# Two tiles' places inside the last output projection, four conditioning steps and the state outputs sooner, another slot ring

## The chip, the core and the metric

The kernel runs on one core of one Trainium2 chip. The metric is the device time of one execution in microseconds (us): 667.77 us is the median of 3 runs of the kernel before (667.08 to 668.85). Engines are named as in the profile: PE (TensorE; PEld is its weight load), DVE (VectorE), ACT (ScalarE), POOL (GpSimd) and SP (SyncE, which issues most of the DMAs).

## The reference

One layer of a hybrid decoder for 256 prompt tokens and 64 sample tokens, all in 32-bit floats: a conditioned projection, two groups of mixing heads, an output projection with a norm behind it, and a mixture of 32 experts of which every token uses two.

```python
def hybrid_layer(x, c, h0, conv0, w_ada, b_ada, ...):
    mod = jax.nn.silu(c) @ w_ada + b_ada
    sh1, sc1, g1, sh2, sc2, g2 = jnp.split(mod[:, None, :], 6, axis=-1)
    h = x * (1.0 + sc1) + sh1
    u, v, xr, yr = jnp.split(h @ w_in, [...], axis=-1)
    v = layer_norm(v, lnv_g, lnv_b)
    out_a = gmlp_spatial(u, v, w_s, b_s)
    xc, conv_new = causal_conv(xr, conv0, conv_w, conv_b)
    hs, h_last = rglru(xc, h0, lru_wa, lru_ba, lru_wx, lru_bx, lru_lam)
    mix = jnp.concatenate([out_a, hs * jax.nn.gelu(yr)], axis=-1) @ w_out
    x = layer_norm(ALPHA * x + (1.0 + g1) * mix, ln1_g, ln1_b)
    h = x * (1.0 + sc2) + sh2
    x = layer_norm(ALPHA * x + (1.0 + g2) * hier_moe(h, ...), ln2_g, ln2_b)
    return x, h_last, conv_new, v

def hier_moe(x, w_rg, b_rg, w_re, b_re, w1, w3, w2):
    gsel = argmax(x @ w_rg + b_rg)                # one group of 8 experts per token
    topv, topi = lax.top_k(le_sel, TOP_K)         # two experts in that group
    wk = softmax(topv) * pgsel
    for e in range(32):
        acc += gate[:, e] * ((silu(x @ w1[e]) * (x @ w3[e])) @ w2[e])
```

The width is 1024, an expert is 512 wide, so its three matrices are 6 MB and all of them 192 MB.

## The kernel before

**Tiles.** The tokens are three tiles: t = 0 and 1 are 128 prompt tokens each, t = 2 the 64 sample tokens. All buffers of weights are 1 MB "slots" of two rings (`slots[0]` with 9, `slots[1]` with 8); a tile that is allocated takes the next buffer of its ring and its first writer waits for the last reader of the tile that was there. PSUM is a ring of 8 banks.

**Order.** The order of every engine's instructions is the order in which the code is written (a manual schedule), and each engine works through its own in order. A wait at one instruction so holds everything behind it on that engine. SP issues the loads of weights in the order of the code too, each when its slot is free.

**Stages around the change.** (1) The projections u, v, xr, yr (L352), with the conditioning of groups 0 to 2 (`ada`, L175) between them. Then the state outputs: four transposes exT (L598), a copy on ACT into a part of a buffer called gx, and four DMA issues on POOL. (2) The output projection, `out_proj(t, n2s)` (L646 on, matmuls L656 and L660): for each tile two halves of 512 columns, eight k each; DVE adds the residual (L664 to L667). (3) `norm(t)` on DVE (L673 to L685) makes the rows h2, whose last step for each half is L682; `turn_h2(t, h)` transposes them on PE (L693), ACT copies them out; `logits(t)` (L703) multiplies with the router's weights; `logits_end` (L707) and `route` (L737 to L751) on DVE pick two experts per token and leave a 0/1 matrix M of token by expert. (4) `count(t)`: two matmuls on M (L763, L764) give, per token and expert, how many tokens came before it, in a PSUM bank pn. `arrange(t)` on DVE (L769 to L775) turns that into places and builds the 0/1 matrix Pd of token by place. `sort(t)` (L857) multiplies h2 with Pd, eight matmuls of 128 columns for tile 2 and of 256 columns for the others (the trace counts two passes for each), and so puts the tokens in the order of their experts; `sorted_out(t)` copies the PSUM banks to xD, in turns on ACT and DVE (L844, L846). (5) `ranks` and "most" (L779 to L887): the largest number of tokens of any expert, which every engine loads into a register. `fetch(0)` copies the first experts' windows xT from xD (L930). All engines then branch on "most" (`tc.If`, L1106). (6) The experts: up (L958), down (L982), combination (L1000). They walk over 200 loads of weights ("we", L639), of which 15 are issued ahead of the branch.

**The last conditioning.** Group 3 (g2, needed only at the very end) has its four loads of two steps each issued in `load_ada2(3)` at L198, its eight steps of four matmuls run by `ada_some(n)` (L175) and its end `ada_end(3)` (L186) on DVE ahead of the branch. `Pd` lies in a slot called "pd" of ring 1, whose first write is a memset of a 128-column strip (L757).

The order of the code from the output projection on, before:

```python
out_proj(2); whiten[2] = norm(2); out_proj(0)
turn_h2(2, 0); turn_h2(2, 1); whiten[0] = norm(0)
out_proj(1, (0,)); logits(2); turn_h2(0, ...); logits(0); route(0 and 2)
out_proj(1, (1,)); count(2); count(0); whiten[1] = norm(1)
ada_some(8); arrange(2); arrange(0)
turn_h2(1, ...); logits(1); logits_end(1); route(1)
sort(2); sort(0, (0, 2)); count(1); sort(0, (4, 6)); arrange(1)
sorted_out(2); sorted_out(0); sort(1); ranks; most; sorted_out(1); ada_end(3)
fetch(0); tc.If(...)
```

Of the kernel before, what the change touches and what calls it, by code (L numbers as in the profile page):

```python
# [17 lines left out]
NE = 32  # L18
# [19 lines left out]
def hymba_step(tc, I, O):  # L38
    nc = tc.nc
    with ExitStack() as ctx:  # L40
# [9 lines left out]
        def slot(name, shape=(128, 2048), dt=F32, i=0):  # L50
            return slots[i].tile(list(shape), dt, name=name, tag="w")
# [50 lines left out]
        gx_ = slot("gx")  # L102
# [90 lines left out]

        def load_ada2(g):
            r = []
            for c in range(4):
                w = slot("wada", (128, 2, 1024))
                nc.sync.dma_start(w, wada[2 * c:2 * c + 2, :, 1024 * (g + 2):1024 * (g + 3)].rearrange("k p n -> p k n"))  # L198
                r += [(2 * c, w[:, 0, :]), (2 * c + 1, w[:, 1, :])]
            return r  # L200
# [321 lines left out]
        for t in range(3):  # L522
# [12 lines left out]
            dst = uT[:, :, TOFF[t]:TOFF[t] + n]  # L535
            V.tensor_tensor(dst, dst, tm, op=OP.mult)
        mb = {}
        mbs = [slot(f"mb{i}", i=1) for i in range(2)]
# [56 lines left out]
        wo = [load_half(wout, 0), load_half(wout, 1)]  # L595
        pex = bank("exT", (36, 512))
        for c in range(4):
            T.transpose(pex[:, c * 128:(c + 1) * 128], ex[:, c, :], ident)  # L598
        exo = gx_[0:36, 1536:2048]
        S.copy(exo, pex)  # L600

        G.dma_start(O["new_h_prompt"][0], exo[0:1, :])
        G.dma_start(O["new_h_sample"][0], exo[1:9, :])
        G.dma_start(O["new_conv_prompt"].rearrange("l b k c -> (l b k) c"), exo[9:12, :])
        G.dma_start(O["new_conv_sample"].rearrange("l b k c -> (l b k) c"), exo[12:36, :])

        G.iota(io256, pattern=[[1, 256]], base=0, channel_multiplier=0, allow_small_or_imprecise_dtypes=True)
# [33 lines left out]
        load_until(4)  # L641
        w_g2 = load_ada2(3)
        V.memset(lg[64:128, 2, :], 0.0)
        st1 = {}

        def out_proj(t, n2s=(0, 1)):  # L646
            n = TW[t]
# [3 lines left out]
            for n2 in n2s:  # L651
                cs = slice(n2 * 512, n2 * 512 + 512)
                p = bank("po")
                if t < 2:
                    for k in range(8):
                        T.matmul(p, abT[k // 4][:, k % 4, ts], wo[n2][k // 4][:, k % 4, :], start=(k == 0), stop=(k == 7))  # L656
                else:
                    for k in range(4):
# [99 lines left out]
        pn = {}  # L758

        def count(t):  # L760

            pn[t] = bank("pn", (128, 2, NE))
            T.matmul(pn[t][:, 0, :], before, M[:, t, :], start=True, stop=True)  # L763
            T.matmul(pn[t][:, 1, :], ones, M[:, t, :], start=True, stop=True)  # L764
# [48 lines left out]
        whiten[2] = norm(2)  # L813
        out_proj(0)
        turn_h2(2, 0)
# [9 lines left out]
        route(slice(0, 3, 2))  # L825
        out_proj(1, (1,))
        count(2)
        count(0)
        whiten[1] = norm(1)
        ada_some(8)  # L830
        arrange(2)
        arrange(0)
        turn_h2(1, 0)
        turn_h2(1, 1)
        logits(1, range(8))


# [22 lines left out]
        def sorted_out(t):  # L860
            W = WID[t]
            per = 512 // W
            for k0 in range(0, 8, per):
                evac(xD[:, k0:k0 + per, XO[t]:XO[t] + W], sorted_.pop((t, k0)))

        logits_end(1)
        route(slice(1, 2))
# [4 lines left out]
        gD = exp.tile([128, NP], F32, name="gD")  # L872
        sort(2)
        sort(0, (0, 2))
        count(1)
        sort(0, (4, 6))
        arrange(1)
        for PT in PT2:
            for cs in (slice(256, 320), slice(384, 448)):
                V.tensor_scalar(PT[:, cs], ident[:, 0:64], 0.0, None, op0=OP.mult)  # L880
        sorted_out(2)
        sorted_out(0)
# [12 lines left out]
        sorted_out(1)  # L895
        ada_end(3)

# [206 lines left out]
        fetch(0)  # L1104
        first = xg[0][1]
        with tc.If(n_most > CAP):  # L1106
            gates_and_windows()
# [165 lines left out]
```

## Time and profile before

| what | value |
|---|---|
| median of 3 runs | 667.77 us (667.08 to 668.85) |
| the profiled execution | 670.56 us |
| its span | 668.7 us |
| PE busy | 591.6 us, 88% |
| DVE busy | 273.0 us, 41% |
| ACT busy | 126.6 us, 19% |
| POOL busy | 52.7 us, 8% |
| DMA, mean | 364 GB/s over the span, 243.57 MB |
| chain of waits | DMA 59%, PE 9%, POOL 1%, DVE 1% |

The page of the profile has one line per engine with its busy time, the span in 40 slices, the chain of work that ended last, and the groups of instructions that cost most. A busy share is a mean over stages with different limits; the chain of waits says which engine or transfer released the next piece of the work that ended last, and the rows of a stretch show what one engine did there, when, and what ended an idle time ahead of it. [...]

### The profile page before, as it was taken

To read this page: it belongs to the slowest core of one execution; us is meant where nothing else is said; L and a number is where in the kernel's file an instruction comes from. 1 tells how busy PE (TensorE), PEld (TensorE's weight loads), DVE (VectorE), ACT (ScalarE), POOL (GpSimd) and SP (SyncE) were. 2 spreads that over 40 slices of the span, in tenths; PEclk is the share of its full clock that TensorE was granted. 3 is DMA by queue.
4 is the path that set the end of the run, shared out by engine and by line. 5 is a ranking of instruction groups with operands and counts; after the bars stand their busy time and mean duration, and the time that the engine had idled before them with its cause. 6 is when DMAs were issued, how large, how long until landed. Compare 5 with 4: busy or idle time off the path is not lost.

```text
span 668.7 us, 7628 instructions
## 1 busy us (share of the span) xinstructions
PE 591.6 (88%) x2767; PEld 271.7 (41%) x2767; DVE 273.0 (41%) x742; ACT 126.6 (19%) x216; POOL 52.7 (8%) x81
## 2 busy tenths in 40 slices
PE   4579999999989999999988989897988979899990
PEld 1377688545743344343332324233332323233330
DVE  0198567694672323323253233232223152323435
ACT  0156371110121101101111111111101010112211
POOL 2031405400000000000010000000000010200003
PEclk9779999999699999999999999999999999999996
DMA  8998859926969999999999999999999999999922
GB/s 328 378 327 311 301 155 311 364 72 240 422 260 419 420 422 421 420 420 420 422 420 421 420 422 421 420 420 421 420 422 420 423 420 421 420 421 421 404 97 79
DMA packets 43949, 243.57 MB, mean 364 GB/s; under 512 B 5678, under 2 KB 6422, under 8 KB 17794
## 3 DMA queue, kind: packets, MB, share of 16 engines
q1 hardware_dynamic: 43106, 242.58, 90.3%
q0 software_dynamic: 800, 0.45, 0.4%
q8 instruction: 23, 0.38, 0.2%
q14 instruction: 20, 0.16, 0.1%
HBM read 241.49 MB, written 1.52 MB: 363 GB/s over the span
## 4 chain that ended last, share of the span: by engine, by line
DMA 59%; PE 9%; POOL 1%; DVE 1%; issue 0%; POOLq 0%; ACT 0%; ACTq 0%; SPq 0%
DMA we<-in_w 59%; PE p L958 6%; PE p L1185 1%; PE pc L1175 1%; POOL xk L1236 0%; PE pc L1000 0%; PE pc L1199 0%; POOLq L1269 0%; POOL xk L1237 0%; PE pgd L908 0%; DVE st L1209 0%; PE ph L970 0%; PE pc L1197 0%; PE pc L1004 0%; PE pr L948 0%
## 5 line engine op out<-in xcount | busy, mean ns | idle before, releaser
L958 PE MATMUL p<-we,xT 128*64 128x512 f32 x1024 | 240.6, 597 | 29.1 <-DMA we<-in_w 26.8
L958 PEld LDWEIGHTS p<-we,xT 128*64 128x64 f32 x1024 | 73.3, 136 | 174.6 <-issue 124.7
L982 PE MATMUL p<-we,hT 128*64 128x512 f32 x480 | 110.0, 596 | 8.0 <-DMA we<-in_w 6.2
L986 DVE TENSOR_TENSOR y<-p,y 64x512 fp32r<-64x512 f32 x60 | 41.3, 689 | 76.7 <-ACT y L985 76.7
L963 ACT ACTIVATE s<-p 64x512 f32<-64x512 f32 x32 | 18.9, 589 | 274.6 <-PE p L958 274.6
L964 DVE TENSOR_TENSOR h<-p,s 64x512 f32<-64x512 f32 x32 | 22.2, 694 | 117.7 <-ACT s L963 117.3
L982 PEld LDWEIGHTS p<-we,hT 128*64 128x64 f32 x480 | 33.5, 137 | 81.4 <-issue 53.2
L930 DVE COPY xT<-xD 128x192 f32 (+1 forms) x96 | 23.6, 248 | 92.7 <-PE p L958 79.0
L985 ACT CAST y<-p 64x512 fp32r<-64x512 f32 x60 | 34.8, 579 | 104.1 <-PE p L982 79.7
L175 PE MATMUL ada<-wada,md 128*32 128x512 f32 (+1 forms) x256 | 27.2, 534 | 6.7 <-DMA wada<-in_w_ada 5.0
L1000 PE MATMUL pc<-y,PT 128*128 128x512 f32 x120 | 32.2, 408 | 0.4 <-DVE y L986 0.2
L1000 PEld LDWEIGHTS pc<-y,PT 128*128 128x128 f32 x120 | 21.3, 188 | 16.4 <-issue 11.4
L352 PE MATMUL pf<-hH,whi 128*128 128x320 f32 x64 | 20.6, 322 | 0.0
L352 PE MATMUL pf<-hL,whi 128*128 128x320 f32 x64 | 19.8, 309 | 0.0
L352 PE MATMUL pf<-hH,wlo 128*128 128x320 f32 x64 | 19.7, 308 | 0.0
L509 POOL PARTITION_BROADCAST g2k<-mod x4 | 1.8, 548 | 196.9 <-PE p L958 196.9
L1004 PE MATMUL pc<-y,PT 128*128 128x512 f32 x60 | 16.2, 392 | 0.0
L656 PE MATMUL po<-wq,uT 128*128 128x512 f32 x32 | 14.7, 601 | 0.0
L857 PE MATMUL px<-pd,h 128*128 128x256 f32 (+1 forms) x48 | 14.4, 471 | 0.1
L656 PE MATMUL po<-wq,ga 128*128 128x512 f32 x32 | 14.4, 592 | 0.0
L970 PEld LDWEIGHTS ph<-ident,h 128*128 128x128 f32 x64 | 9.0, 209 | 12.0 <-issue 7.9
L293 DVE TENSOR_TENSOR wlo<-wq,whi 128x1024 fp32r<-128x1024 f32 x12 | 13.9, 1218 | 0.0
(323 smaller groups left out, 586.5 us busy)
## 6 DMA issues: line engine op xcount, KB each, us to landing
we<-in_w SPq DMA_DIRECT2D x188, 1024.0 KB, 19.8
wada<-in_w_ada SPq DMA_DIRECT2D x24, 1024.0 KB, 5.3
wq<-in_w_in SPq DMA_DIRECT2D x8, 1024.0 KB, 9.2
wq<-in_w_out SPq DMA_DIRECT2D x4, 1024.0 KB, 5.4
we<-in_w SPq DMA_DIRECT2D x8, 512.0 KB, 11.5
xk<-in_x_prompt SPq DMA_DIRECT2D x1, 1024.0 KB
out_y_prompt<-xk SPq DMA_DIRECT2D x4, 256.0 KB
xk<-in_x_sample SPq DMA_DIRECT2D x1, 256.0 KB
```

The lines of the kernel that those rows point to most:

```text
L175: T.matmul(ada_p[g][32 * j:32 * j + 32, :], cT[:, k, :], wj, start=(k == 0), stop=(k == 7))
L352: T.matmul(p, w[k // 4][part][:, k % 4, f * 128:(f + 1) * 128], x[:, k, :], start=(i == 0 and k == 0), stop=(i == 2 and k == 7))
L656: T.matmul(p, abT[k // 4][:, k % 4, ts], wo[n2][k // 4][:, k % 4, :], start=(k == 0), stop=(k == 7))
L930: V.tensor_copy(xT[:, :, BASE[t]:BASE[t] + CAPS[t]], xD[:, :, XO[t]:XO[t] + WID[t] + CAPS[t]][:, :, bass.ds(v, CAPS[t])])
L958: T.matmul(p[64 * q:64 * q + 64, :], xT[:, k, :], w(q, k), start=(k == 0), stop=(k == 7))
L963: S.activation(s[64:128, :], p[0:64, :], AF.Silu)
L964: V.tensor_tensor(h[64 * a:64 * a + 64, :], p[64:128, :], s[64:128, :], op=OP.mult)
L982: T.matmul(p[q], hT[:, k, sl], w(q, k), start=(k == 0), stop=(k == 3))
L985: S.copy(yg[0][sl, cs], p[q])
L986: V.tensor_tensor(yg[1][sl, cs], p[q], yg[0][sl, cs].bitcast(F32), op=OP.subtract)
L1000: T.matmul(pc[t, q], PT[:, TOFF[t]:TOFF[t] + 128], yg[i][:, H[q]], start=False, stop=stop and i == 1)
L1004: T.matmul(pc[2], PT[:, cs], yg[i][:, H[q]], start=False, stop=False)
```

## The change

Six things change, and no arithmetic. (a) The four exT transposes, their copy and the four state outputs are written ahead of the last projection rather than behind it; the last quarter of the output weights thereby takes the buffer gx. (b) `load_ada2(3, 1)` takes its four slots from ring 1 rather than ring 0, so "pd", the next on that ring, takes another buffer. (c) `ada_some(4)` stands between the halves of out_proj(0), and the other four steps one by one in the sorting of tile 2, ahead of the logits of tile 1 and behind the first half of tile 0's sorting. (d) `out_proj` gets a hook `between`, which runs behind the third of the eight k: the counts of tiles 2 and 0 (now in one PSUM bank) and their arrangements stand inside the last output projection. (e) The sorting of tile 2 stands behind norm(1) and ahead of turn_h2(1), and its copies to xD are issued ahead of arrange(1). (f) `ada_end(3)` stands behind fetch(0).

```diff
-        def load_ada2(g):
+        def load_ada2(g, i=0):
...
-                w = slot("wada", (128, 2, 1024))
+                w = slot("wada", (128, 2, 1024), i=i)
...
+        pex = bank("exT", (36, 512))
+        for c in range(4):
+            T.transpose(pex[:, c * 128:(c + 1) * 128], ex[:, c, :], ident)
+        exo = gx_[0:36, 1536:2048]
+        S.copy(exo, pex)
...
-        w_g2 = load_ada2(3)
+        w_g2 = load_ada2(3, 1)
...
-        def out_proj(t, n2s=(0, 1)):
+        def out_proj(t, n2s=(0, 1), between=None):
...
                         T.matmul(p, abT[k // 4][:, k % 4, ts], wo[n2][k // 4][:, k % 4, :], start=(k == 0), stop=(k == 7))
+                        if k == 2 and between:
+                            between()
...
-            pn[t] = bank("pn", (128, 2, NE))
+            if t < 2:
+                pn[t] = bank("pn", (128, 2, NE)) if t else pn[2, 0]
+            else:
+                both = bank("pn", (128, 2, 2, NE))
+                pn[2], pn[2, 0] = both[:, 0], both[:, 1]
...
-        out_proj(0)
+        out_proj(0, (0,))
+        ada_some(4)
+        out_proj(0, (1,))
...
-        out_proj(1, (1,))
-        count(2)
-        count(0)
-        whiten[1] = norm(1)
-        ada_some(8)
-        arrange(2)
-        arrange(0)
-        turn_h2(1, 0)
-        turn_h2(1, 1)
-        logits(1, range(8))
...
+        def between():
+            for t in (2, 0):
+                count(t)
+            for t in (2, 0):
+                arrange(t)
+
+        out_proj(1, (1,), between)
+        whiten[1] = norm(1)
+        sort(2, (0,))
+        ada_some(1)
+        sort(2, (4,))
+        ada_some(1)
+        turn_h2(1, 0)
+        turn_h2(1, 1)
+        ada_some(1)
+        logits(1, range(8))
...
-        sort(2)
+        sorted_out(2)
         sort(0, (0, 2))
+        ada_some(1)
         count(1)
...
-        sorted_out(2)
...
-        ada_end(3)
...
         fetch(0)
         first = xg[0][1]
+        ada_end(3)
```

On PE, from the last output projection to the first zero passes ahead of the branch, the order before (po is the output projection, pn the counts, p the transposes of h2, pr the logits, px the sorting; lines of before):

```order
L656 MATMUL po<-wq,ga 128x512 x4
L763 LDWEIGHTS mm
L763 MATMUL pn<-M,mm 128x32
...
L175 MATMUL ada<-wada,md 32x256 x32
L693 MATMUL p_1365<-ident,h_1064 128x128 x4
...
L703 MATMUL pr<-wr,ga 128x40 x4
L857 MATMUL px<-pd,h_1064 128x128 x8
L857 MATMUL px<-pd,h_1064 128x256 x4
...
L764 MATMUL pn<-M,mm 128x32
L857 MATMUL px<-pd,h_1064 128x256 x12
```

And the same stretch of PE after (its lines are some 2 to 6 further down in the code):

```order
L656 MATMUL po<-wq,uT 128x512 x3
L769 LDWEIGHTS mm
L769 MATMUL pn<-M,mm 128x32
...
L656 MATMUL po<-wq,ga 128x512 x4
L854 MATMUL px<-pd,h_1074 128x128 x4
L175 MATMUL ada<-wada,md 32x256 x4
...
L695 MATMUL p_1366<-ident,h_1074 128x128 x4
...
L705 MATMUL pr<-wr,ga 128x40 x4
L854 MATMUL px<-pd,h_1074 128x256 x4
L175 MATMUL ada<-wada,md 32x256 x4
...
L854 MATMUL px<-pd,h_1074 128x256 x12
```

The eight sorting matmuls px of tile 2 have moved ahead of tile 1's transposes, the block of 32 conditioning passes is gone, with groups of four in the places named under (c), and the counts of tiles 2 and 0 stand within the projection. 

On DVE, behind the rows that spread the conditioning over the tokens (mb), up to tile 2's norm, with the semaphores that each row waits for, before:

```order
L511 STREAM_SHUFFLE mb_865<-md 32x256 x7
L643 MEMSET lg 64x40
L726 MEMSET one_1137 128x32
L757 MEMSET pd 128x128
L664 TENSOR_TENSOR po<-po,md 64x512 [waits Activation_49]
```

And the same rows of DVE after:

```order
L643 MEMSET lg 64x40
L728 MEMSET one_1137 128x32
L759 MEMSET pd 128x128 [waits DMAHW4_49,PE_49]
L666 TENSOR_TENSOR po<-po,md 64x512 [waits Activation_49]
L667 TENSOR_TENSOR po<-po,mb_875 64x512 [waits DVE_49]
```

The memset of pd keeps its place in DVE's order and has gained a wait for a load and for PE.

## Rows read from the trace of the kernel before

**Rows 1.** The chain of waits: start in us, us, what; from 222 on.

```profile
222.92 17.91 DMA we<-in_w
...
602.19 19.82 DMA we<-in_w
```

**Rows 2.** Windows: stretch, then busy us (count) of five engines, PEclk, DMA, GB/s.

```profile
180.00:200.00 20.00, 17.94 (x83) 10.40 (x83) 14.83 (x61) 5.33 (x9) 0.76 (x6) 0.97 0.74 287
```

**Rows 3.** Timeline of SP, 194 to 195: start, us, engine, line, operation.

```profile
194.58 0.35 SPq L639 DMA_DIRECT2D we<-in_w  x1
```

**Rows 4.** Timeline of PE, 122 to 158; the bracket is idle time before.

```profile
123.70 0.61 PE L598 MATMUL exT<-ident,gx 128*36 128x128 f32 x4
...
138.23 3.60 PE L656 MATMUL po<-wq,uT 128*128 128x512 f32 x8
...
145.19 0.71 PE L693 MATMUL p<-ident,h 64*128 64x64 f32 x8
145.83 3.70 PE L656 MATMUL po<-wq,uT 128*128 128x512 f32 x8
...
155.28 1.08 PE L703 MATMUL pr<-wr,uT 128*128 128x40 f32 x8 [0.24 <-ACT uT L694]
156.20 1.06 PE L703 MATMUL pr<-wr,ga 128*128 128x40 f32 x8
157.09 3.68 PE L656 MATMUL po<-wq,uT 128*128 128x512 f32 x8
```

**Rows 5.** Timeline of PE, 164 to 192, up to the first expert's passes.

```profile
164.22 3.66 PE L175 MATMUL ada<-wada,md 128*32 128x256 f32 x64
168.96 1.29 PE L693 MATMUL p<-ident,h 128*128 128x128 f32 x8 [1.07 <-DVE h L682]
...
173.05 7.92 PE L857 MATMUL px<-pd,h 64*128 64x128 f32 x24
...
180.86 6.61 PE L857 MATMUL px<-pd,h 128*128 128x256 f32 x24
187.41 1.26 PE L994 MATMUL pc<-mm,zero 1*128 1x256 bf16 x10
190.18 1.94 PE L958 MATMUL p<-we,xT 128*64 128x512 f32 x8 [1.51 <-DVEq L1106]
```

**Rows 6.** Timeline of DVE, 133 to 189.

```profile
133.11 0.17 DVE L757 MEMSET pd<- 128x128 f32 x1
...
140.57 1.40 DVE L682 SCALAR_TENSOR_TENSOR h<-h,mvo,mb 64x512 f32<-64x512 f32 x2
...
159.59 0.22 DVE L751 TENSOR_TENSOR M<-oh 128x64 bf16<-128x64 f32 x1
...
169.65 0.21 DVE L769 TENSOR_TENSOR_SCAN offs<-one,pn 128x32 f32<-128x32 f32 x1
...
173.50 0.19 DVE L707 TENSOR_TENSOR lg<-pr,brt 128x40 f32<-128x40 f32 x1
...
175.42 0.19 DVE L751 TENSOR_TENSOR M<-oh 128x32 bf16<-128x32 f32 x1
181.06 0.22 DVE L769 TENSOR_TENSOR_SCAN offs<-one,pn 128x32 f32<-128x32 f32 x1 [5.45 <-PE pn L764]
...
183.48 1.88 DVE L846 COPY xD<-px 128x512 f32<-128x512 f32 x3
...
186.22 0.25 DVE L887 TENSOR_REDUCE most<-over 128x1 int32<-128x96 f32 x1
187.15 1.29 DVE L846 COPY xD<-px 128x512 f32<-128x512 f32 x2 [0.68 <-PE px L857]
```

**Rows 7.** Windows of 2 us, columns as in rows 2, PEclk third from the end.

```profile
170.00:172.00 2.00, 1.99 (x15) 1.75 (x14) 1.69 (x9) 0.79 (x2) 0.00 (x0) 0.79 0.99 410
...
180.00:182.00 2.00, 2.00 (x9) 1.59 (x8) 0.82 (x4) 0.00 (x0) 0.00 (x0) 0.65 1.01 422
188.00:190.00 2.00, 0.67 (x7) 0.34 (x4) 1.33 (x5) 1.40 (x2) 0.20 (x3) 1.00 0.97 393
```

More of the change, by code (lines that the diff above doesn't have):

```diff
@@ L536, in hymba_step @@
             V.tensor_tensor(dst, dst, tm, op=OP.mult)
+        pex = bank("exT", (36, 512))
[3 more added lines that the diff above has]
+        S.copy(exo, pex)
+        G.dma_start(O["new_h_prompt"][0], exo[0:1, :])
+        G.dma_start(O["new_h_sample"][0], exo[1:9, :])
+        G.dma_start(O["new_conv_prompt"].rearrange("l b k c -> (l b k) c"), exo[9:12, :])
+        G.dma_start(O["new_conv_sample"].rearrange("l b k c -> (l b k) c"), exo[12:36, :])
         mb = {}
@@ L595, in hymba_step @@
         wo = [load_half(wout, 0), load_half(wout, 1)]
[L596 to L605, printed above, removed]
         G.iota(io256, pattern=[[1, 256]], base=0, channel_multiplier=0, allow_small_or_imprecise_dtypes=True)
```

## The prediction

> **What bounds the kernel now.** I read the chain of waits first. From 222.92 us on, nearly everything in it is the stream of expert weights: one entry of some 18 to 20 us follows another until 622.01 [rows 1]. A chain of transfers that long means that the end of the kernel is a fixed distance from the moment at which that stream got going; whatever starts the stream 1 us sooner or later moves the end by 1 us. So the second view is the stretch around the start. Between 180 and 200 us the DMA engines are busy only 0.74 of the time [rows 2]: the fifteen pieces that may be loaded ahead of the branch are issued, and the first load behind the branch is issued at 194.58 [rows 3]. It waits for a slot, that is for the first sixteen expert passes, which start at 190.18 [rows 5]; 194.58 - 190.18 = 4.40 us lie between. The start of the experts therefore sets the time.
>
> What sets that start? The PE row at 190.18 has waited 1.51 us for DVE's branch [rows 5]. On DVE ahead of it stand the copies xD from 187.15, the windows xT and, 3.7 us before 190.18, the end of "most" (186.22 + 0.25 = 186.47) [rows 6]. The same distance from the other side: the last sorting pass ends where the zero passes begin, 187.41, and 2.77 us later the experts start [rows 5]. I use both, 3.71 us behind "most" and 2.77 us behind the last pass, and the later one counts. Going back from "most": three copies from 183.48, tile 1's arrangement from 181.06, and there the row to see: DVE has waited 5.45 us for tile 1's count on PE [rows 6]. The places that it counts were ready at 175.42 + 0.19 = 175.61 [rows 6], but on PE the count stands behind 24 sorting passes that take 7.92 us [rows 5]. Those passes ran at half clock: the granted clock is 0.79 in 170 to 172 and 0.65 in 180 to 182 [rows 7], which puts the fall at 171.16 (a part of the 2 us at 1.00, the rest at 0.50) and the return at 181.4, 10.24 us in all, 2.2 us after PE had waited 1.07 us for tile 1's normalised rows at 168.96 [rows 5].
>
> **The state outputs sooner.** Four transposes (0.61 us, [rows 4]) stand before the projection of wy rather than behind it. They only change places on PE, and neither their copy on ACT nor the four POOL issues is on the path. The last quarter of the output weights now takes the buffer that these transfers read, so it waits for them; they stand a whole projection sooner, and only the second half of tile 2's output projection needs that quarter. I take 0; the bounds are 0 below, since nothing behind them gets shorter, and above what that quarter is late (rival 3).
>
> **The other ring, and a wait that it adds.** The last four conditioning loads go to slots of the shorter ring, and the expert pieces behind them on SP's queue find the other slots. I take 0 for the stream, because it comes to rest ahead of the branch anyway: the 15th piece has until the experts reach it. But "pd", on the same ring, now gets the buffer of conditioning steps 0 and 1 and its memset waits for PE to have used it. In the kernel before that memset ran at 133.11 and waited for nothing [rows 6]. Now steps 0 and 1 stand behind the first half of out_proj(0), which ends at 138.23 [rows 4]; the eight steps take 3.66 us [rows 5], so two take 0.92, and the memset runs at 139.15, 6.04 us later. DVE is in order, and behind that memset stands tile 2's norm. In the kernel before its rows ended at 140.57 + 1.40 = 141.97 [rows 6]; now 148.0. PE reaches tile 2's transposes at 145.19 + 1.83 (four steps) = 147.0, waits 1.0, and goes on with out_proj(1) at 148.6 in place of 145.83 [rows 4]: +2.7 us for everything behind it. Without the wait it would be +1.83.
>
> **Counts and arrangements inside the last output projection.** It starts at 157.09 + 2.7 = 159.8. After three of its eight k (7.1 us from 157.09 to the row behind it at 164.22, counts included, so 2.6, [rows 4, 5]) the counts of tiles 2 and 0 come at 162.4; their M is ready at 159.59 + 0.22 + 2.7 = 162.5 [rows 6], so the new wait on PE is 0.1 to 0.3. The two arrangements (169.65 to 173.50, 3.85 us, [rows 6]) then run on DVE from 163.0 to 166.9 under the other 4.3 us of the projection, which ends at 167.2, 3.0 after the 164.2 of before. They leave the place between tile 1's norm and its logits at no cost. Norm(1) starts with the end of the projection, so tile 1's transposes start at 168.96 + 3.0 = 172.0.
>
> **What fills the shadow of norm(1).** Before: eight conditioning steps, 3.66 us, then 1.07 idle. After: the sorting of tile 2 and two steps. Sixteen of the 24 half-clock passes are of tile 2 and half as wide; at full clock all 24 would take 3.96, so tile 2's take about 1.95, plus 0.92 = 2.9 us, from 167.2 to 170.1. PE then idles 1.9 us. Behind it: transposes 1.29 [rows 5], one step 0.46, logits 1.98 at full clock (two rows like 155.28, which starts 0.92 before the next, [rows 4]), then half of tile 0's sorting, one step, the count of tile 1. So what stood in front of the count falls from 24 passes to 8 and a step.
>
> **The sum with the clock held.** Logits end 172.0 + 1.29 + 0.46 + 1.98 = 175.75. DVE took 2.11 us from its logits row at 173.50 to M [rows 6]; M is ready at 178.0, the count at 178.2, where PE has been done since 178.2 as well (8 passes at 0.25 and a step 0.46). DVE has one copy of tile 2 first (0.63 of the 1.88 for three), arranges until 180.75, then the two constant rows (0.41), two copies (1.25), ranks and "most" (1.1 from the copies' end at 183.48 + 1.88 to 186.47, [rows 6]): 183.5, so experts at 187.2. The sixteen passes of tile 1 run from 180.8 to 184.75 (24 take 6.61, [rows 5]); with 2.77 behind them 187.5. That is 2.7 sooner than 190.18: 665.1 us.
>
> **The sum with the clock falling as before.** The level fell 2.2 us after the end of a 1.07 us wait behind 3.66 us of narrow conditioning passes. After the change PE meets the same sequence, narrow or half-height passes, a longer wait (1.9), transposes, logits. So the level should fall at 172.0 + 2.2 = 174.2, within the logits: they end at 177.1 rather than 175.75, the eight passes take 3.6 more to 180.75, the step 0.9, the count comes at 181.8 and tile 1 is arranged at 184.0. "Most" ends at 186.8, +0.3. On PE: if the level lasts 10.24 us as before, until 184.4, tile 0's other eight passes end at 185.1, tile 1's sixteen at 188.85, and with 2.77 behind them the experts start at 191.6, +1.4. If it came back a third sooner, near 181, the same sum gives 187.7 for the passes and +0.3. The only length that the trace has is 10.24, so I stay near that end: +1.1. The gain of having fewer passes ahead of the count is then eaten by starting 3 us later. The profiled execution took 670.56, 1.86 around its span of 668.7; by it 671.7. It stood 2.79 over the median of the runs, 667.77, to which I apply the shift: 668.9.
>
> [...] At 168.96 a pause of 1.07 us was followed by half clock, at 190.18 one of 1.51 us was not, since 188 to 190 still shows 1.00 [rows 5, 7]. [...]
>
> **The rivals.**
> 1. The clock holds (chance 0.28): 665.1, between 664.2 and 665.8. For it: tile 2's sorting passes are wider than the conditioning steps that they replace, one more step stands ahead of the logits, and the longer pause at 190.18 brought no fall. Against: the pause is 0.8 longer than the one at 168.96.
> 2. The fall comes at the experts (chance 0.10), the slower side. The cover of the start is ten zero passes of 1.26 us and a 1.51 us wait [rows 5]. If the level falls in this stretch, the sixteen passes ahead of the first slot, 3.9 us at full clock (1.94 for eight), double: +3.9 on the +1.1, 672.8; with a fall half way, +1.9, 670.8. It decides once PE's work before 190 is thinner than before; against it stands that the last sixteen passes stay where they were.
> 3. The change does not do what it says, or a load is late (chance 0.06): the output weights behind the state outputs, or the memset's wait longer than 6 us. Each microsecond that out_proj(2) stalls delays all behind it by one, while the level falls the same way: 669.5 to 671.
>
> **How the numbers follow.** The forecast, a clock that falls again, has 0.56 and its own range 667.3 to 669.8: -0.5 where PE's wait is shorter and the level returns early, +2.0 where it lasts 10.24 us and the counts wait 0.5 longer. 0.3% of 667.77 is 2.0 us, about what a measurement of this kernel can tell from no change; it leaves 665.8 to 669.8 as "same". Rival 1 lies just under it, nearly whole: faster 0.28. The forecast lies in it but for 0.03. Slower is rival 2 (0.10), rival 3 (0.04 of 0.06) and that 0.03: 0.17. Same is the rest, 0.55. The range for 8 in 10 takes in most of rival 1 and reaches to the lower end of rival 2 and most of rival 3: 664.4 to 670.6.
>
> **What would show it.** In the trace after: the "pd" memset at 139 or later with an idle time before it that PE ended; the wait on PE before tile 2's transposes, about 1 us; arrangements of tiles 2 and 0 between 163 and 167; PE's wait before tile 1's transposes of 1.9 us ending near 172; the granted clock at 174 to 176 (0.5 to 0.6 by the forecast, 1.00 by rival 1) and at 190 to 194 (1.00, or less by rival 2); the idle time of DVE before tile 1's arrangement, 5.45 before, about 3 by the forecast and near 0 with the clock held; and the first load behind the branch, 194.58 before, at 195.7 by the forecast, 191.9 by rival 1. I would be wrong if that load moved and the end did not, or if the memset did not wait.

## The result and the profile after

The changed kernel takes 674.39 us (median of 20 runs, 668.75 to 676.45), the kernel before 668.55 (20 runs, 667.08 to 672.13). The ratio is 1.0065 with a 95% interval of 1.0049 to 1.0082: slower by some 4.3 us. The ratio is not that of the two medians, which lie 5.8 us apart; by either, the time is above the predicted range (664.4 to 670.6). Out of the ratios below are left one run of e5 (763.60 us) and one of e7 (690.73), in a slow state of the chip with a granted clock of 0.75 and 0.84 of full speed. The profiled execution took 675.74 us with a span of 673.6, against 670.56 and 668.7 before and 671.7 forecast.

Two traces can't be laid over each other by their times alone. In the trace of before TensorE ran at half clock early on (PEclk, the granted clock as a share of full speed, is 0.50), in that of after it did not (1.00). The windows of the same 2 us, before and after (columns as in [rows 2]):

```profile
42.00:44.00 2.00, 2.00 (x9) 2.00 (x8) 2.00 (x7) 0.00 (x0) 0.94 (x2) 0.50 1.04 403
```

```profile
42.00:44.00 2.00, 2.00 (x15) 1.76 (x15) 2.00 (x6) 0.97 (x3) 1.21 (x3) 1.00 1.04 387
```

So I count from a mark in code that the change leaves alone, the last sixteen conditioning passes between the projections. They start at 122.70 in before and at 120.23 in after (timeline of PE, as in [rows 4]):

```profile
122.70 1.07 PE L175 MATMUL ada<-wada,md 128*32 128x256 f32 x16
```

```profile
120.23 1.07 PE L175 MATMUL ada<-wada,md 128*32 128x256 f32 x16
```

The rest of PE's timeline after, up to the experts; the bracket is idle time before a row:

```profile
145.93 1.16 PE L695 MATMUL p<-ident,h 64*128 64x64 f32 x8 [1.61 <-DVE h L684]
147.02 5.21 PE L656 MATMUL po<-wq,uT 128*128 128x512 f32 x8
...
167.13 2.18 PE L854 MATMUL px<-pd,h 64*128 64x128 f32 x8
169.81 2.29 PE L854 MATMUL px<-pd,h 64*128 64x128 f32 x8
...
173.03 1.97 PE L695 MATMUL p<-ident,h 128*128 128x128 f32 x8
...
193.46 7.07 PE L970 MATMUL p<-we,xT 128*64 128x512 f32 x24 [1.55 <-DVEq L1119]
```

The first rows answer to those of tile 2's transposes and the projection behind them in [rows 4]: 0.71 us without a wait and 3.70 us there, a wait of 1.61, then 1.16 and 5.21 us here. Behind the last projection stand tile 2's sorting passes, where [rows 5] have the conditioning and an idle 1.07. Counted from the mark, the end of the projection comes 46.90 us on (167.13 - 120.23) against 41.52 before (164.22 - 122.70, [rows 5]), the experts 73.23 against 67.48. So 5.4 of the 5.8 us that the experts lose are lost by the end of the projection. Of the first load behind the branch, on SP:

```profile
198.84 1.70 SPq L639 DMA_DIRECT2D we<-in_w  x2
```

It is issued 78.61 us behind the mark, against 71.88 [rows 3]: +6.7, where I had forecast +1.1. The end of the span is 553.4 behind it against 546.0: +7.4. The chain of waits is the stream as before [rows 1], only later: the first of its entries behind 222 starts at 227.19 rather than 222.92.

The granted clock has three low stretches after, one before ([rows 7]; it is 0.50 there from 172 to 181). The last number but two of each window:

```profile
148.00:150.00 2.00, 2.00 (x4) 0.94 (x3) 1.93 (x4) 0.00 (x0) 0.00 (x0) 0.50 0.91 324
170.00:171.00 1.00, 1.00 (x5) 1.00 (x6) 1.00 (x3) 0.00 (x0) 0.00 (x0) 0.78 0.00 0
182.00:184.00 2.00, 2.00 (x11) 0.54 (x10) 0.34 (x1) 0.74 (x2) 0.00 (x0) 0.50 1.02 430
184.00:185.00 1.00, 1.00 (x9) 0.91 (x6) 0.57 (x3) 0.00 (x0) 0.00 (x0) 0.89 0.70 295
195.00:197.00 2.00, 2.00 (x8) 0.83 (x6) 1.58 (x9) 1.65 (x4) 0.00 (x0) 0.50 0.00 0
```

By narrower windows it is low from 146.7 to 150.1, from 170.6 to 184.2 (13.7 us, where before had 10.24) and from 194.5 to 197.9, among the first experts' passes.

DVE after, the rows that answer to [rows 6]:

```profile
128.82 0.42 DVE L600 TENSOR_TENSOR ini<-md,lnm 128x256 f32<-128x256 f32 x1 [7.02 <-DMA lnm<-in_ln_b]
...
137.58 0.17 DVE L759 MEMSET pd<- 128x128 f32 x1
...
145.04 1.40 DVE L684 SCALAR_TENSOR_TENSOR h<-h,mvo,mb 64x512 f32<-64x512 f32 x2
...
162.85 0.22 DVE L775 TENSOR_TENSOR_SCAN offs<-one,pn 128x32 f32<-128x32 f32 x1 [0.34 <-PE pn L770]
...
184.36 0.22 DVE L775 TENSOR_TENSOR_SCAN offs<-one,pn 128x32 f32<-128x32 f32 x1 [2.02 <-PE pn L770]
```

The first row is the surprise: DVE waits 7.02 us for "lnm", a small load of the norm's scale and shift that the change does not touch. The kernel before did not wait for it. That wait is also why the memset of pd has no bracket. POOL issues that load; its timeline before and after:

```profile
104.80 2.21 POOL L509 PARTITION_BROADCAST mb<-md  x4 [23.17 <-DVE md L182]
...
110.60 2.05 POOL L560 DMA_DIRECT2D lnm<-in_ln_g  x4
```

```profile
103.56 0.53 POOL L543 DMA_DIRECT2D out_new_h_prompt<-gx  x1 [23.45 <-DVE uT L536]
...
105.11 0.52 POOL L546 DMA_DIRECT2D out_new_conv_sample<-gx  x1
114.28 1.80 POOL L509 PARTITION_BROADCAST mb<-md  x4 [8.66 <-issue]
...
117.78 2.05 POOL L571 DMA_DIRECT2D lnm<-in_ln_g  x4
```

After, the four state outputs stand ahead of POOL's first broadcast. By the code they wait for ACT's copy, which ends at 103.26 (the bracket names DVE, whose row ends at 103.56). The first is issued at 103.56, and nothing behind them on POOL began sooner; the last issue ends at 105.63, and then 8.66 us go by in which POOL waited for nothing that the profile shows. The broadcast's data were there at 101.83. Before, they were there at 104.65, and the same broadcast started 0.15 us later: whatever those 8.66 us are, they seem to have gone by within the 23.17 us in which POOL waited for DVE. The lnm loads are issued 7.2 us later, or 9.65 counted from the mark.

### The profile page after: what moved, and what is told of

The parts are those of the page before. It is cut to its first block, busy times and chain, and to the rows that moved or that the text cites. A ratio compares the mean times of both kernels' runs of the same rounds, so it can differ in the third digit from the quotient of the medians.

```text
span 673.6 us, 7623 instructions
## 1 busy us (share of the span) xinstructions
PE 596.2 (89%) x2767; PEld 273.9 (41%) x2767; DVE 272.4 (40%) x742; ACT 126.7 (19%) x216; POOL 53.3 (8%) x81
## 4 chain that ended last, share of the span: by engine, by line
DMA 59%; PE 9%; POOL 1%; DVE 1%; issue 0%; POOLq 0%; ACT 0%; ACTq 0%; SPq 0%
DMA we<-in_w 59%; PE p L970 6%; PE p L1198 1%; PE pc L1188 1%; POOL xk L1249 0%; PE pc L1012 0%; PE pc L1212 0%; POOLq L1282 0%; POOL xk L1250 0%; PE pgd L920 0%; DVE st L1222 0%; PE ph L982 0%; PE pc L1210 0%; PE pc L1016 0%; PE pr L960 0%
## 5 line engine op out<-in xcount | busy, mean ns | idle before, releaser
L970 PEld LDWEIGHTS p<-we,xT 128*64 128x64 f32 x1024 | 75.0, 137 | 174.4 <-issue 124.3
L656 PE MATMUL po<-wq,uT 128*128 128x512 f32 x32 | 16.5, 659 | 0.0
L175 PEld LDWEIGHTS ada<-wada,md 128*32 128x32 f32 x256 | 6.1, 113 | 19.7 <-DMA wada<-in_w_ada 11.2
```

Source lines behind the costliest of these rows:

```text
L175: T.matmul(ada_p[g][32 * j:32 * j + 32, :], cT[:, k, :], wj, start=(k == 0), stop=(k == 7))
L970: T.matmul(p[64 * q:64 * q + 64, :], xT[:, k, :], w(q, k), start=(k == 0), stop=(k == 7))
```

## The experiments

**How they are compared.** Each kernel's profiled execution is one draw of a clock that varies between executions of one kernel (its mean goes from 0.965 to 0.986 in the 20 runs of after), so the verdicts are the ratios of the timed runs to runs of before beside them; the traces show the mechanism. The table gives, from the traces, how much later (+) or sooner (-) than in before each point comes, in us counted from the mark (before: projection's end 41.52, tile 1's transposes 46.26, experts 67.48, first load behind the branch 71.88, span's end 546.0). In after, e1, e5 and e6 the state transposes, 0.6 us, lie ahead of the mark, so their columns are too low by that.

| kernel | projection's end | transposes | experts | first load | span's end | median us | ratio to before |
|---|---|---|---|---|---|---|---|
| after | +5.4 | +6.5 | +5.8 | +6.7 | +7.4 | 674.39 | 1.0065 |
| e1 | +5.6 | +5.6 | +4.2 | +5.4 | +5.8 | 674.97 | 1.0071 |
| e2 | +3.3 | +3.9 | -1.9 | -1.0 | -0.2 | 667.58 | 0.9989 |
| e3 | +2.3 | +3.3 | -1.3 | -0.6 | +0.1 | 668.76 | 0.9998 |
| e4 | 0.0 | 0.0 | -0.9 | +1.1 | +0.6 | 668.65 | 1.0002 |
| e5 | +2.7 | +3.3 | -2.5 | -1.7 | -1.9 | 670.37 | 1.0007 |
| e6 | +2.7 | +3.8 | +3.0 | +4.0 | +4.0 | 669.84 | 1.0004 |
| e7 | +0.2 | +2.8 | -2.0 | +3.0 | +2.6 | 669.98 | 1.0023 |
| e8 | +0.2 | +1.7 | -4.0 | +1.0 | +0.4 | 668.76 | 0.9997 |
| e9 | +0.2 | +1.3 | -2.3 | -1.6 | -1.9 | 667.20 | 0.9972 |
| e10 | +0.2 | +0.5 | -2.1 | -0.8 | -1.2 | 668.14 | 0.9980 |

In all of them the end moves with the first load behind the branch, to within 0.9 us. The experts' start is not as good a measure, as e7 and e8 show.

**e1: the kernel before with part (a) alone.**

```diff
             V.tensor_tensor(dst, dst, tm, op=OP.mult)
+        pex = bank("exT", (36, 512))
...
+        S.copy(exo, pex)
+        G.dma_start(O["new_h_prompt"][0], exo[0:1, :])
...
         mb = {}
...
         wo = [load_half(wout, 0), load_half(wout, 1)]
-        pex = bank("exT", (36, 512))
...
```

> The kernel before with one part of the change: transposes, copy and state outputs ahead of the last projection. Theory Q (POOL's queue): POOL's first broadcast and the lnm loads come some 8 us later, DVE waits about 7 us for lnm as it did after (7.02), tile 2's rows are ready near 149 instead of 142, and PE, with no conditioning step there, waits about 3.5 us ahead of tile 2's transposes: 3 to 6 us slower than before, more if the clock falls behind that wait. Theory K (the clock alone): the queue's delay is hidden, no wait of PE over 0.5 us there, and the time is that of before within 1 us.

1.0071 (1.0047 to 1.0096): the whole loss of the change. POOL and PE of e1:

```profile
107.89 0.52 POOL L546 DMA_DIRECT2D out_new_conv_sample<-gx  x1
116.56 1.80 POOL L509 PARTITION_BROADCAST mb<-md  x4 [8.16 <-issue]
...
120.07 2.06 POOL L571 DMA_DIRECT2D lnm<-in_ln_g  x4
```

```profile
148.33 1.26 PE L693 MATMUL p<-ident,h 64*128 64x64 f32 x8 [3.30 <-DVE h L682]
149.52 5.94 PE L656 MATMUL po<-wq,uT 128*128 128x512 f32 x8
```

The same gap of 8 us on POOL, the wait of DVE for lnm (6.68 us), a wait of 3.30 on PE, and then the transposes and half of out_proj(1) at half clock: 5.94 us rather than 3.70. The clock is low from 147.2 to 154.1, and again from 181.4 to 184.8 and from 195.0 to 198.4. The wait of 3.30, 0.55 more on the transposes and 2.24 on the projection are 6.1 us, which is the 5.6 of the table at the projection's end with the 0.6 of the state transposes added.

**e2: the changed kernel without part (a).** The edit is that of e1 turned round: (b) to (f) stay.

> The kernel after with the state outputs back in their old place. Theory Q: DVE waits nothing for lnm, but the memset of pd now waits for the first two conditioning steps (to about 139.2, an idle time of 5 to 6 us ended by PE), so PE's wait ahead of tile 2's transposes stays near 1.0 against 1.6 after; about 1 us faster than after. Theory K: within 1 us of after, with the same low stretch of 13 us in the shadow of norm(1).

0.9989 (0.9962 to 1.0015). DVE and PE of e2:

```profile
136.70 0.17 DVE L759 MEMSET pd<- 128x128 f32 x1 [6.37 <-PE ada L175]
```

```profile
145.05 0.43 PE L695 MATMUL p<-ident,h 64*128 64x64 f32 x4 [0.55 <-DVE h L684]
...
164.67 2.17 PE L854 MATMUL px<-pd,h 64*128 64x128 f32 x8
...
167.34 2.16 PE L854 MATMUL px<-pd,h 64*128 64x128 f32 x8
...
170.00 1.09 PE L695 MATMUL p<-ident,h 128*128 128x128 f32 x8
```

Without the late loads the wait of the memset for the conditioning appears as forecast. PE waits 0.55 and a further 0.23 for tile 2's rows, the clock stays at 1.00 from 130 to 200, and PE is never idle ahead of tile 1's transposes. The experts come 1.9 us sooner, the end by 0.2. The expectation had the kernel only about 1 us faster than the changed one, since PE's wait gets just 0.8 shorter; by the two ratios it is 0.76%, some 5 us. The rest fits the low stretches of after's trace, 20.5 us in all, which e2's doesn't have.

**e5 and e6: the place of the four issues.** Both keep the transposes and the copy where the change put them, and move the four issues on POOL alone: in e5 behind the loads of lnm and of the router's weights, in e6 just behind POOL's first broadcast, still ahead of those loads.

```diff
         S.copy(exo, pex)
-        G.dma_start(O["new_h_prompt"][0], exo[0:1, :])
...
         spread("g1", 1, (range(4), slice(0, 256)))
+        G.dma_start(O["new_h_prompt"][0], exo[0:1, :])
...
```

(the edit of e6)

> The kernel after, transposes and copy still ahead of the last projection, but POOL issues the four state outputs behind the lnm and wr loads. If their place on POOL's queue is the cause, POOL's first broadcast comes without the idle time of 8 us, DVE waits nothing for lnm, the memset of pd is the wait again (about 6 us, ended by PE, as in e2) and the time is that of e2 within 1 us: 666.5 to 668.5, 6 faster than after. If the early transposes or the copy on ACT cost it, it stays within 2 us of after.

> The kernel after, POOL's four state outputs behind its first broadcast of the conditioning (g1), but still ahead of the lnm loads and of the output weights' last quarter. If what costs is the broadcast's start-up of about 8 us held behind the outputs' wait for ACT's copy, it is hidden again: the lnm loads are issued only some 2 to 3 us later than before, DVE waits under 2 us for them, and the time is within 1.5 us of e5. If four more transfers on that queue cost it, DVE still waits 4 us or more and the time is over 671.

1.0007 (0.9977 to 1.0036) and 1.0004 (0.9977 to 1.0031): either place takes the loss away. POOL and DVE of e6:

```profile
104.94 2.21 POOL L509 PARTITION_BROADCAST mb<-md  x4 [23.17 <-DVE md L182]
106.98 0.71 POOL L550 DMA_DIRECT2D out_new_h_prompt<-gx  x1
...
110.84 1.05 POOL L571 DMA_DIRECT2D lnm<-in_ln_g  x2
```

```profile
124.85 0.43 DVE L600 TENSOR_TENSOR ini<-md,lnm 128x256 f32<-128x256 f32 x1
```

Four issues ahead of the lnm loads cost nothing that DVE sees; it is the broadcast's start behind them that does. Nor does an issue ahead of any broadcast cost 8 us. In e5 another one (L575) stands right behind the four issues and starts at once:

```profile
117.06 0.35 POOL L575 PARTITION_BROADCAST brt<-bias  x1
```

So it is not the four issues or their transfers, but the 8 us ahead of POOL's first broadcast of the conditioning (8.66 in after, 8.16 in e1), which a waiting issue holds back. e5 was expected at the time of e2 within 1 us and came 0.18% above it by the ratios; the intervals overlap widely.

e6 tells a second thing. In its profiled execution the clock fell at 171.0, with half clock until 184.6, and the experts were 3.0 us late:

```profile
172.00:174.00 2.00, 2.00 (x14) 0.97 (x14) 0.95 (x4) 0.00 (x0) 0.00 (x0) 0.50 0.00 0
```

e2's and e5's traces, with the same order of work on PE in this stretch, hold 1.00 from 140 to 205; tile 1's transposes take 1.09 us in both and 1.97 in e6. Here is e2:

```profile
170.00:171.00 1.00, 1.00 (x12) 0.86 (x8) 0.23 (x3) 0.31 (x1) 0.00 (x0) 1.00 0.00 0
```

So this fall is not fixed by the order of the code. The median of e6 is 669.84 although its profiled execution took 674.94; its runs go from 666.19 us at a mean granted clock of 0.985 to 674.94 at 0.972.

**e3: no wait of the memset either.** e2, with the memset of `onef` (the 128-column strip of pd, L759) written behind norm(0).

```diff
-        V.memset(onef, 1.0)
...
         whiten[0] = norm(0)
+        V.memset(onef, 1.0)
```

> As e2, and the memset of a strip of pd written behind tile 0's norm, so that it holds nothing. Theory Q: no wait of PE ahead of tile 2's transposes and no low clock near 147, which were 1.6 and about 1.6 us after: 3 to 4 us faster than after, 1 to 3 slower than before, since four conditioning steps (1.8 us) lie on PE's path and the level still falls near 170. Theory K: the wait is gone and the time is that of after within 1 us.

0.9998 (0.9975 to 1.0022). The wait is gone, PE doesn't wait for tile 2's rows, and the projection ends 1.0 us sooner than in e2 (the column at +2.3). Nothing of that arrives: in this trace the clock fell for 3.4 us from 169.1, with 1.97 us for tile 1's transposes rather than e2's 1.09, and again from 186.1. It was expected 1 to 3 us slower than before and is not. The wait that the other ring adds is real and is worth less than a comparison can tell.

**e4: the pause on PE filled.** The kernel before, with one matmul of 512 columns in the idle 1.07 us behind the conditioning [rows 5]; its result goes into a bank that nobody reads.

```diff
         ada_some(8)
+        wide(1)
         arrange(2)
```

> The kernel before with one matmul of 128 rows by 512 columns (about 0.9 us, its result unused) behind the eight conditioning steps, in the 1.07 us in which PE waits for tile 1's norm. If the pause brings the fall at 171, the clock stays at 1.00 there, the 24 sorting passes take about 4 us and the experts start 3 to 4 us sooner: 664 to 665. If the narrow work of the conditioning steps brings it, pause or no pause, the level falls between 168 and 172 all the same: the time of before within 1 us.

1.0002 (0.9978 to 1.0026). PE of e4, and a window:

```profile
165.02 1.12 PE L814 MATMUL wide<-h,ident 128*128 128x512 f32 x2
166.15 1.23 PE L693 MATMUL p<-ident,h 128*128 128x128 f32 x8
```

```profile
172.00:174.00 2.00, 2.00 (x8) 1.78 (x8) 0.69 (x5) 0.58 (x1) 0.00 (x0) 0.50 1.02 418
```

PE ran through without the pause, with no wait in its rows from 157.81 to the fall, and the clock fell all the same at 170.4, until 177.3. The fall therefore doesn't need the pause ahead of tile 1's transposes: this trace has a fall with no wait in front of it.

**e7 and e8: conditioning steps later.** Both drop (a) and (b) and the four steps inside out_proj(0), and move steps towards the end of the sorting, e7 with wide matmuls between tile 2's sorting passes, e8 without.

```diff
         sort(2, (0,))
-        ada_some(1)
+        ada_some(2)
         sort(2, (4,))
-        ada_some(1)
+        ada_some(2)
...
         sort(1)
+        ada_some(3)
```

(e8; e7 has one step and `wide(1)` at the first two places, two steps ahead of count(1) and four behind sort(1))

> State outputs, ring and conditioning loads as before; counts and arrangements of tiles 2 and 0 inside the last projection, tile 2's sorting in the shadow of norm(1) with two conditioning steps and two matmuls of 128 by 512 (result unused) so that PE is never idle and less of its work is narrow; two steps behind tile 0's first sorting, four behind tile 1's. No memset wait, no steps on PE's path. Clock held: experts start near 184.5 in a trace that starts like the one of before, 662.5 to 664. If narrow work lowers the clock all the same, 665.5 to 667.

> As e7 without the two unused wide matmuls: four steps in the shadow of norm(1), one behind tile 0's first sorting, three behind tile 1's. If the share of narrow work there decides the clock, its level falls more often than in e7 and it is 1 to 3 us slower than e7; if not, both agree within 0.7 us.

1.0023 (1.0004 to 1.0042) and 0.9997 (0.9979 to 1.0015), although the clock stays at 1.00 from 160 to 200 in both and the experts start sooner by 2.0 and 4.0. The waits of SP in e7 (sum, count, longest) and a window of e7:

```profile
SPq L639 <- PE ada L175: 12.2, 2, 6.7
```

```profile
194.00:196.00 2.00, 2.00 (x12) 0.94 (x10) 0.75 (x3) 0.00 (x0) 0.00 (x0) 1.00 0.34 66
```

The late steps hold slots, expert pieces that could be loaded ahead wait 12.2 us for them (16.3 in e8), and the DMA engines stand at 0.34 of their time just where the stream should run. The first load behind the branch, in order on SP, is 3.0 and 1.0 us later than before. No slot of the experts seems to hold it: it is issued 9.4 us behind the experts' start in both, over twice the 4.40 of before. SP stands at the branch itself:

```profile
SPq L1124 <- SPq L1124: 9.4, 3, 5.7
```

(e7; one wait of 5.0 in before.) The pieces issued late are still under way then; that SP waits for them to land fits the times, but the view names no transfer. Both kernels missed what was expected of them, e7 by 3 us (662.5 to 667), and e8, without the wide matmuls, was not slower than e7 but 1.2 us faster.

**e9 and e10: the loads on time.** e9 keeps (d) and (f), drops (a) and (b), and runs four steps right behind the projection and four behind half of tile 2's sorting, whose other half stands behind tile 1's logits. All of tile 0's sorting comes behind the count of tile 1. e10 puts wide passes of tile 0's sorting between the steps in place of tile 2's narrow ones: four passes, 1.33 us, which is a quarter of that sorting and not the half that its expectation names.

```diff
         whiten[1] = norm(1)
+        ada_some(4)
         sort(2, (0,))
-        ada_some(1)
-        sort(2, (4,))
-        ada_some(1)
+        ada_some(4)
         turn_h2(1, 0)
         turn_h2(1, 1)
-        ada_some(1)
         logits(1, range(8))
...
+        sort(2, (4,))
         sorted_out(2)
```

> State outputs, ring and conditioning loads as before; counts and arrangements inside the last projection; in the shadow of norm(1) four conditioning steps, half of tile 2's sorting, four steps, so that PE never idles and the slots of the steps are free by 171 as before; the other half of tile 2's sorting behind the logits, then the count of tile 1. Theory (PE is full behind the projection, and only its pause of 1.07, the waits and the low clock can be won; the loads ahead of the branch must not be held): no second hole in the stream, experts 3 us sooner than before where the clock holds: 664.5 to 666.5. If the level falls as often as before: 667 to 668.5.

> As e9, with half of tile 0's sorting (128 rows, 256 columns) between the steps in place of half of tile 2's (64 rows, 128 columns), and tile 2's behind it. If rows and columns of the passes between the steps decide whether the level falls, it holds more often than in e9 and the time is 1 to 2 us lower; if not, both agree within 0.7 us.

e9: 667.20 us, 0.9972 (0.9948 to 0.9995), against 669.22 for the runs of before beside it. By that it is faster than before by 0.28%, but the interval only just leaves out 1, which among ten comparisons can be chance; by the two ratios it is faster than the changed kernel by 0.9%. e10: 668.14, 0.9980 (0.9960 to 0.9999). PE of e9, SP's wait, and the windows of 168 to 200:

```profile
169.13 1.93 PE L175 MATMUL ada<-wada,md 128*32 128x256 f32 x32
171.00 1.09 PE L695 MATMUL p<-ident,h 128*128 128x128 f32 x8
```

```profile
SPq L639 <- PE ada L175: 2.1, 1, 2.1
```

```profile
168.00:176.00 8.00, 7.76 (x69) 6.43 (x69) 4.16 (x16) 1.07 (x3) 0.00 (x0) 1.00 1.01 421
176.00:180.00 4.00, 3.89 (x13) 3.21 (x13) 3.31 (x14) 1.17 (x2) 0.00 (x0) 0.57 1.02 424
...
182.00:200.00 18.00, 15.65 (x77) 9.14 (x77) 11.90 (x49) 4.75 (x8) 0.76 (x6) 1.00 0.80 317
```

With the steps back near their old place SP waits 2.1 us, the DMA share behind 182 is 0.80, and the end moves with the experts. The clock still fell for 3.4 us. That the wide passes of e10 would keep the clock up better than the narrow ones of e9 is not borne out by the times: in its trace the clock held until 190.9 and fell then, and it is 0.9 us slower.

## Why the prediction was wrong, point by point

**The step that failed: "I take 0" for the state outputs.** I wrote that neither the copy nor the four POOL issues is on the path, and bounded them only by the output weights behind them on SP (rival 3). The issues stand in POOL's order, and I did not ask what stands behind them there: the broadcasts, whose 8 us without a visible row seem to have been hidden in a wait of 23.17 us, and the loads of lnm, which DVE reads ahead of tile 2's norm. In place of 0, (a) alone costs the whole loss (e1: 0.71%, some 4.7 us); e2, e5 and e6, without that order, lose nothing measurable. Rival 3 named the class, a late load, but on the wrong queue and at 669.5 to 671 rather than 674.4.

**How 8 us on POOL became some 5 us of the kernel.** Tile 2's rows come little later than with the memset's wait alone: 145.04 - 120.23 = 24.8 us behind the mark, or 25.4 with the state transposes, in e2 144.17 - 119.87 = 24.3. But PE waits 1.61 us rather than 0.78, and from there on runs at half clock, which costs 0.45 on the transposes and 1.51 on the first half of out_proj(1). PE waited 1.61 and 3.30 us here in after and e1, and the clock fell; in e2, e5 and e6 it waited 0.55 to 0.78, and the clock held. That is two traces against three, not a rule: with a wait of 1.51 to 1.56 us ahead of the experts the clock fell there in six traces (after, e1, e3, e4, e6, e10) and held in four (before, e2, e5, e9). The other part of the loss in after's trace is the second low stretch and the third; the second came in e6's trace without the first. That the first makes the others likelier fits the times (above 671.5 are 17 of 20 runs of after, 11 of 12 of e1, 4 of 20 of before, 2 of 12 of e2 and 4 of 12 of e6), but no run shows the link. That most of the loss comes with a low clock is what the list of after's runs suggests: the two with a mean granted clock of 0.985 and 0.986 took 668.8 us, about the time of before, and the other 18, at 0.978 or less, 669.8 to 676.5.

**The memset's wait was right and was covered.** 6.04 forecast, 6.37 measured in e2; in after the lnm wait of 7.02 came first, and by 137.58 the two steps were done. For e2 the projection's end was forecast at +3.0 and came at +3.3.

**The 0 for the stream held, though loads were late.** With the new ring and places the steps hold slots longer, and SP waits 20.5 us for a step ahead of the branch, where in before it waited 0.2:

```profile
SPq L639 <- PE ada L175: 20.5, 1, 20.5
```

The first 64 expert passes still ran without a wait, and the first load behind the branch waited for their first sixteen, as before.

**Counts and arrangements inside the projection: right as a mechanism.** The scan starts with a wait of 0.34, inside the projection. That its time, 162.85, is near the forecast 163.0 is luck: counted from the mark it is 42.6 us, 2.3 later than forecast. DVE's wait ahead of tile 1's arrangement falls from 5.45 [rows 6] to 2.02 (about 3 forecast). As a gain it was worth little, since the path was full elsewhere.

**Tile 2's sorting was mis-sized.** I split the time of 24 passes by columns and took 1.95 us for tile 2's sixteen. At full clock they take 2.17 + 2.16 = 4.3 us in e2, 0.27 each, while tile 0's passes, twice as wide, take 2.26 for eight, 0.28 each. So the passes don't get shorter with their width here. Nor were tile 2's any slower at half clock: 4.2 us for the sixteen in before, at 0.50 from 173 to 177. PE's weight loads for them fill nearly all of the time, 3.90 us for sixteen at half clock in before, 1.98 for eight at full clock in e2:

```profile
173.04 3.90 PEld L857 LDWEIGHTS px<-pd,h 64*128 64x128 f32 x16
```

```profile
164.67 1.98 PEld L854 LDWEIGHTS px<-pd,h 64*128 64x128 f32 x8 [0.76 <-issue]
```

Of the 24 passes the low stretch had lengthened only tile 0's eight, so there was less to win than the sum had. The idle 1.9 us that I put ahead of tile 1's transposes doesn't exist, they come 0.9 later in e2 than the sum had them (+3.9 rather than +3.0), and "PE idles" was no longer a sign to look for. A second term is off in the sum itself: tile 1's sixteen passes, put at 180.8 to 184.75, take 4.4 us by the 6.61 for 24 from which they were taken. Rival 1's gain is then 2.2 us rather than 2.7, and the forecast's loss on PE 2.1 rather than 1.4.

**The clock fell, but not for the reason given.** I tied the fall to the pause. (The row of 188 to 190, given for a pause without a fall, lies ahead of the experts; the clock did stay at 1.00 behind it, to 205.) In after the second fall starts at 170.6, in the middle of full work, 24 us after PE's last wait of over 0.3 us (145.93); e4 has it without a pause; and e2, e5 and e6 differ between executions of one order. What brings it stays open. Rival 2's fall at the experts did come in after's trace, where 64 passes of the chain took 15.65 us rather than the 14.67 of before (1.94 + 0.49 + 12.24); but in e2, at 1.00, they took 15.47 (1.94 + 1.29 + 12.24), so little of the difference need be the clock's. Nor is its condition, thinner work on PE, borne out: e4, with before's order and one matmul more, had the fall too. In e2 rival 1 came true on PE, with the experts 1.9 us sooner (2.7 forecast), but the kernel as a whole did not gain from it.

**"1 us sooner at the experts is 1 us sooner at the end" was half right.** It holds for the first load behind the branch, within 0.9 us in eleven traces. Between the experts' start and that load I had counted on the 4.40 us of before; it is 5.1 to 5.2 in e2, e3, e5 and e9 (190.71 - 185.50 in e2), some 0.7 more, 5.4 to 6.4 in after, e1, e4, e6 and e10, where the clock fell there, and 9.4 in e7 and e8. In e2 the 0.8 more is one idle time of PE behind the first eight passes, 1.29 us rather than 0.49, which ends with nothing that the profile shows. Of the gain of (b) to (f), 1.3 to 2.5 us at the experts in e2, e3 and e5, at most 1.9 arrives in a trace and nothing measurable in the times.

## What to carry to other kernels

Before an instruction that waits is put ahead of another on an in-order queue, look at what the other's idle time hides: a wait of 23.17 us for data seems to have covered a start of 8.16 to 8.66 us on POOL, and a DMA issue in front of it, which waits for something else, laid that start bare. Ask of the whole queue behind it which small load some other engine will miss. And where loads take turns with compute in a ring of slots, work that frees slots should stay early: the two orders that moved it late won up to 4 us at the experts and gave it all back.

## What the runs showed of the hardware

The first broadcast on POOL behind elementwise work (TENSOR_TENSOR rows) started after 8 to 9 us without a row: 8.66 in after, 8.16 in e1. It is not the first of the kernel (one stands at 52.50 in after, also behind such a row, and started after 9.28 us), and a broadcast with only memsets and DMA issues between it and another broadcast had no such gap (117.06 in e5, 118.37 in before). What the 8 to 9 us consist of, no run shows.

Sorting passes of 128 columns on 64 rows cost 0.27 us each, those of 256 columns on 128 rows 0.28 (e2); the weight loads of the first fill 3.90 of 4.2 us for sixteen at half clock (before) and 1.98 of 2.17 for eight at full (e2). And the granted clock differs between executions of the same order of work in three places: in the first 50 us (0.50 in before and 1.00 in after from 42 to 44), where after's trace was 2.5 us ahead of before's at the mark; near 170 (0.50 in e6 and 1.00 in e2 from 172 to 174), from which on e6 lost 5 us that e2 did not; and at the experts' start, where it fell in six traces of ten with the same wait of 1.51 to 1.56 us.
